# A new order for the attention's steps, and one norm's gain product cut between POOL and VectorE

## The chip, the cores and the metric

The kernel runs on one core of a Trainium2 chip. The metric is the device time of one execution in microseconds (us); lower is better. Engines are written as in the profile: PE is TensorE's matmul, PEld its weight load, DVE is VectorE, ACT is ScalarE, POOL is GpSimd, SP is SyncE, which issues the DMAs.

## The reference, cut to what matters

Input and output are 256 rows of 1024 float32. Two layers run in turn; each has a half SwiGLU block (an FFN of width 2816), a mixer, and another half SwiGLU block, each with a norm in front and a norm behind:

```
for i in range(2):
    f = swiglu(rms_norm(x, g[0]), ...);            x = x + 0.5 * rms_norm(f, g[1])
    h = rms_norm(x, g[2])
    m = pool_mixer(h, ...) if i == 0 else nsa_mixer(h, ...)
    x = x + rms_norm(m, g[3])
    f = swiglu(rms_norm(x, g[4]), ...);            x = x + 0.5 * rms_norm(f, g[5])
```

`rms_norm(x, g)` is `x * rsqrt(mean(x*x) + eps) * g`. The mixer of layer 0 is linear in h up to a bias (causal means over 2, 4, 8 and 16 rows, then a product with a 256 x 256 matrix for each of four groups of columns), so that the row factor of its norm may be multiplied in later. The mixer of layer 1 is an attention with 16 heads in 4 groups: one projection of h gives queries, three pairs of keys and values, and gates; one pair is compressed (blocks of 32 rows through a small two-layer network), and each query attends to the compressed keys, to selected blocks and to a window. At 256 rows all blocks are selected, so the second and the third branch are plain causal softmaxes. The three outputs are weighted by the gates and projected.

## The kernel before, in words

The 256 rows are two tiles of 128 rows, t = 0 and 1. Weights come from HBM as float32 pieces (`raw`, four buffers of 128 x 1024). Each is split in two float32r parts, `hi` by a copy on ACT (L295) and `lo` by a subtraction on VectorE (L296); a product takes three matmuls, hi by hi, hi by lo and lo by hi (`mm3`, L304 to L307). The weight tiles `whi` and `wlo` have three buffers, so the next piece can be split only when a matmul group has let one go.

The stages follow each other in `_trunk`: `ffn`, `pool_mixer`, `ffn`, `ffn`, `nsa`, `ffn`. In front of each stands an object of the class `Pre` (L369 to L401), which makes the normed and transposed input of the stage for each row tile. `Pre(2, False)` belongs to the pooling mixer: it multiplies x by the gain alone (`scaled`, L355, two halves of 512 columns, both on VectorE, L358), computes the row factor `r` beside it (`rstd`), and transposes on PE (L365); `r` is applied after the group matmuls (L606, L607). The others multiply by gain and row factor in one instruction a half (L394). `post` (L345) is the norm behind a stage; its L351 writes x half by half.

The attention stage, `nsa`, is a list of steps, `NSA_STEPS`, each a kind with two indices, which `step` (L950) carries out by tracing instructions. The kinds that matter here:

- `load c h` brings half h of projection chunk c and splits it; `proj c t` multiplies it by row tile t (24 matmuls). Chunks 3 and 5 are the queries, 4 the values of the two plain branches.
- `q c t` copies eight heads' queries out of PSUM (L783); `nope c t` transposes them (L789); `rope c t` rotates their first 16 columns in place by small VectorE operations (L683 to L688), splits them in hi and lo (L311) and transposes both (L803). The writes of L687 and L688 wait for the transposes of `nope`, which read the same tile.
- `cmp`, `hid`, `kcmp`, `vcmp` compress keys and values. `cmp_mm` is 64 small matmuls in the trace (L745); `cmp_k` ends with two VectorE copies to `kbd` (L766); `cmp_v` starts with two copies to `rep` (L772). `pc c t` is the softmax over compressed keys (L814 on), `pct` its transpose.
- `qk t g` is the plain softmax of group g, in four calls: scores of two heads' two branches and their exponentials, then a scaling, then both again for the other two heads. A score step takes two of the four PSUM banks called `acc`: scores and mask on PE (L855, L857), maximum on VectorE (L859), exponentials on ACT (L861), which set the banks free. The scaling is on POOL (L869, L870).
- `pv t g` transposes the weights (L893) and multiplies them by the values (L880), with a masked copy on POOL (L906).
- `wo i` brings a quarter of the output projection and splits it in four pieces of 512 columns: hi on ACT, lo on POOL (`eng=nc.gpsimd`, L988). `out t h` multiplies by it.

What sets the order: the code is traced once, and a planner (`schedule_with_timeline_sim=True`) lays the instructions out on each engine. It runs through its own estimate of the times; at each point an engine gets, of the instructions whose inputs and buffers its estimate has ready, the one that was traced first. The place in `NSA_STEPS` is thus a priority, not the place on the engine. On the chip each engine works off its queue in the order that the planner left, and waits at an instruction whose inputs are late, with all that stands behind it. Blocks under `urgent` have a raised priority, and `after` adds an order by hand.

Of the kernel before, what the change touches and what calls it, by code (L numbers as in the profile page):

```python
# [13 lines left out]
OP = mybir.AluOpType  # L14
# [22 lines left out]
NSA_STEPS = [  # L37
    ("kpost", 0, 0),
    ("load", 1, 0),
    ("wcmp", 0, 0),  # L40
    ("load", 1, 1),
    ("load", 4, 0),
    ("cpost", 0, 0),
    ("load", 4, 1),
    ("load", 3, 0),
    ("proj", 0, 1),
    ("proj", 1, 0),
    ("proj", 4, 0),
    ("cpost", 0, 1),
    ("load", 3, 1),  # L50
    ("kpost", 0, 1),
    ("proj", 1, 1),
    ("cmp", 0, 0),
    ("proj", 3, 0),
    ("cpost", 1, 0),
    ("cpost", 1, 1),
    ("proj", 4, 1),
    ("gates", 0, 0),
    ("q", 0, 0),
    ("load", 5, 0),  # L60
    ("hid", 0, 0),
    ("nope", 0, 0),
    ("proj", 3, 1),
    ("wcmp", 1, 0),
    ("vpost", 0, 1),
    ("cmp", 1, 0),
    ("kcmp", 0, 0),
    ("pc", 0, 0),
    ("q", 0, 1),
    ("rope", 0, 0),  # L70
    ("load", 5, 1),
    ("proj", 5, 0),
    ("nope", 0, 1),
    ("qk", 0, 0),
    ("hid", 1, 0),
    ("qk", 0, 0),
    ("pc", 0, 1),
    ("q", 1, 0),
    ("pct", 0, 0),
    ("proj", 5, 1),  # L80
    ("qk", 0, 1),
    ("rope", 0, 1),
    ("qk", 0, 1),
    ("vcmp", 0, 0),
    ("qk", 0, 0),
    ("qk", 1, 1),
    ("qk", 0, 0),
    ("q", 1, 1),
    ("qk", 1, 0),
    ("nope", 1, 0),  # L90
    ("pct", 0, 1),
    ("vpost", 0, 0),
    ("pv", 0, 0),
    ("nope", 1, 1),
    ("qk", 1, 0),
    ("pc", 1, 0),
    ("rope", 1, 0),
    ("pv", 0, 0),
    ("pv", 0, 0),
    ("qk", 0, 1),  # L100
    ("pc", 1, 1),
    ("qk", 0, 1),
    ("pv", 0, 1),
    ("pct", 1, 0),
    ("qk", 1, 0),
    ("pv", 0, 1),
    ("qk", 0, 2),
    ("qk", 1, 0),
# [5 lines left out]
    ("rope", 1, 1),
    ("vcmp", 1, 0),
    ("qk", 1, 1),
    ("pv", 1, 0),
    ("qk", 1, 1),
    ("qk", 0, 3),
    ("qk", 1, 1),  # L120
    ("pv", 1, 1),
    ("pv", 1, 0),
    ("pv", 1, 1),
    ("qk", 0, 2),
    ("qk", 0, 3),
    ("wo", 0, 0),
    ("qk", 0, 2),
    ("qk", 1, 2),
    ("qk", 1, 3),
    ("qk", 1, 3),  # L130
    ("pv", 1, 1),
    ("qk", 0, 2),
    ("pv", 1, 1),
    ("qk", 0, 3),
    ("pv", 0, 2),
    ("pct", 1, 1),
    ("out", 0, 0),
    ("pv", 0, 2),
    ("pv", 1, 1),
    ("qk", 1, 2),  # L140
    ("qk", 1, 3),
    ("qk", 1, 2),
    ("pv", 0, 3),
# [3 lines left out]
    ("pv", 0, 2),
    ("qk", 1, 2),
    ("wo", 1, 0),
    ("pv", 0, 3),  # L150
# [3 lines left out]
    ("out", 0, 1),
    ("pv", 1, 2),
    ("wo", 2, 0),
    ("pv", 1, 2),
    ("wo", 3, 0),
    ("pv", 1, 3),
    ("pv", 1, 2),  # L160
# [77 lines left out]
def _trunk(ctx: ExitStack, tc: tile.TileContext, d, out):  # L238
    nc = tc.nc
# [5 lines left out]
    x = [pp.tile([P, DM], F32, name=f"x{t}") for t in range(NT)]  # L245
# [11 lines left out]
    rope = csm[:, 290:322].rearrange("p (t n) -> p t n", t=NT)  # L257
# [11 lines left out]
    H = [slice(h * 512, (h + 1) * 512) for h in range(2)]  # L269
# [61 lines left out]

    def rstd(src, half, t):
        s = pp.tile([P, 2], F32, name=f"ssq{t}", bufs=2)
        k = 4.0 if half else 1.0
        for h in range(2):
            j = pp.tile([P, 512], BF16, name="junk", bufs=1)
            nc.scalar.activation(j, src[h], AF.Square,
                                 scale=(2.0 if half else 1.0) / 32.0, accum_out=s[:, h:h + 1])
        v = pp.tile([P, 1], F32, name=f"ms{t}", bufs=2)
        nc.vector.tensor_scalar(v, s[:, 0:1], s[:, 1:2], EPS * k, op0=OP.add, op1=OP.add)  # L340
        r = pp.tile([P, 1], F32, name=f"rs{t}", bufs=2)
        nc.gpsimd.tensor_tensor(r, v, neghalf, op=OP.pow)  # L342
        return r
# [8 lines left out]
            if last:  # L352
                nc.sync.dma_start(out[t * P:(t + 1) * P, H[h]], x[t][:, H[h]])

    def scaled(t, g):  # L355
        xg = fx[t]
        for h in range(2):
            nc.vector.tensor_mul(xg[:, H[h]], x[t][:, H[h]], g[:, H[h]])  # L358
        return xg

    def transposeT(src, dst):
        for h in range(2):
            pt = psG.tile([P, 4, P], F32, name="g")
            for k in range(4):
                i = nc.tensor.transpose(pt[:, k, :], src[:, (4 * h + k) * P:(4 * h + k + 1) * P], ident)  # L365
            r = split([q[:, 4 * h:4 * h + 4, :] for q in dst], pt)
        return r, i

    class Pre:  # L369
        def __init__(self, n, normed=True):  # L370
            self.n, self.normed, self.g, self.xT, self.xx, self.r, self.h, self.T = n, normed, None, None, None, {}, {}, {}

        def load(self):
# [3 lines left out]
        def emit(self, t):  # L377
            if t in self.r:
                return
            self.load()  # L380
            if self.xT is None:
                self.xx = pp.tile([P, 2, KD, S], F32R, name="xT")
                self.xT = tuple(self.xx[:, i] for i in range(2))
            with urgent(t):
                if self.n == 0:
                    self.r[t] = r = rstd(halves(x[t]), False, t)
                    xg = fx[t]
                    self.s = [nc.vector.scalar_tensor_tensor(xg[:, H[h]], x[t][:, H[h]], r, self.g[h], op0=OP.mult, op1=OP.mult)
                              for h in range(2)]
# [653 lines left out]
```

## Time and profile before

| | |
|---|---|
| median of 3 runs | 943.79 us (943.63 to 943.89) |
| the profiled execution | 944.33 us, of it 942.5 us span |
| busy in the span | PE 922.8, PEld 771.4, DVE 634.5, ACT 466.2, POOL 84.3 us |
| granted TensorE clock | 0.996 of full speed |

The span runs from the first to the last instruction that the profiler recorded. Busy time is the union of the instructions of an engine; what is left of PE's span, 19.7 us, are its waits. The order of the stages in the span, read off the lines in the timeline: the first FFN to about 198 us, the pooling mixer to 213, the next two FFNs to 584, the attention to 750, and the last FFN.

### The profile page before, as it was taken

What the parts mean: (1) busy time and instruction counts of PE and PEld (TensorE: products, weight loads), DVE (VectorE), ACT (ScalarE), POOL (GpSimd) and SP (SyncE); (2) the same over time, 40 slices, a digit from 0 to 9 for tenths busy, and PEclk for the clock granted to TensorE, in tenths of its full rate; (3) what the DMA queues carried; (4) which work ended last, traced back from release to release, by engine and by line L of the source; (5) the groups of instructions that cost most, each with busy time, mean ns of one, the idle gap of its engine ahead of it and who ended that gap; (6) DMA issues with size and microseconds to landing.
All of it is one profiled execution on the core that took longest, in us unless ns stands there. A gap on an engine that the chain in (4) does not pass through costs nothing.

```text
span 942.5 us, 13047 instructions
## 1 busy us (share of the span) xinstructions
PE 922.8 (98%) x4922; PEld 771.4 (82%) x4922; DVE 634.5 (67%) x899; ACT 466.2 (49%) x792; POOL 84.3 (9%) x104
## 2 busy tenths in 40 slices
PE   8999999999999999999999999999899999999997
PEld 5888888877888888878888888877776688888886
DVE  5866776786867667558576666775863668666653
ACT  6643644364744444446454444544874565544421
POOL 0003000110000000000000000002667100000000
PEclk9999999999999999999999999999899999999999
DMA  8865765334866656248665662835200358665511
GB/s 317 287 217 165 261 225 183 110 131 157 269 244 192 206 175 224 97 133 277 217 223 180 195 207 63 307 140 179 90 1 27 107 190 296 204 211 185 188 45 45
DMA packets 48021, 168.96 MB, mean 179 GB/s; under 512 B 5587, under 2 KB 6099, under 8 KB 47958
## 3 DMA queue, kind: packets, MB, share of 16 engines
q1 hardware_dynamic: 47958, 168.12, 53.4%
q8 instruction: 39, 0.64, 0.3%
q14 instruction: 24, 0.20, 0.1%
HBM read 167.05 MB, written 1.05 MB: 178 GB/s over the span
## 4 chain that ended last, share of the span: by engine, by line
PE 94%; DVE 3%; ACT 2%; issue 1%; DMA 0%; POOL 0%; DVEq 0%; POOLq 0%; SPq 0%; ACTq 0%
PE g L504 28%; PE g L505 15%; PE acc L305 9%; PE acc L307 9%; PE acc L306 9%; PE g L305 5%; PE g L306 5%; PE g L307 5%; PE g L472 2%; PE g L365 1%; PE g L880 1%; PE g L893 1%; PE g L745 1%; PE acc L855 1%; ACT big L861 1%
## 5 line engine op out<-in xcount | busy, mean ns | idle before, releaser
L504 PE MATMUL g<-xT,whi 128*128 128x512 f32 x1152 | 406.1, 394 | 0.0
L505 PE MATMUL g<-xT,wlo 128*128 128x256 f32 x1152 | 325.1, 282 | 0.0
L295 ACT ACTIVATE whi<-raw 128x1024 fp32r<-128x1024 f32 (+2 forms) x252 | 204.8, 862 | 159.1 <-issue 43.3
L296 DVE TENSOR_TENSOR wlo<-raw,whi 128x1024 fp32r<-128x1024 f32 (+2 forms) x236 | 230.8, 1020 | 47.5 <-ACT whi L295 47.1
L504 PEld LDWEIGHTS g<-xT,whi 128*128 128x128 f32 x1152 | 216.3, 188 | 49.6
L505 PEld LDWEIGHTS g<-xT,wlo 128*128 128x128 f32 x1152 | 216.5, 188 | 1.4
L296 DVE TENSOR_TENSOR dlo<-raw,dhi 128x1024 fp32r<-128x1024 f32 (+1 forms) x128 | 119.4, 954 | 95.3 <-ACT dhi L295 95.2
L295 ACT ACTIVATE dhi<-raw 128x1024 fp32r<-128x1024 f32 (+1 forms) x128 | 103.9, 841 | 146.2 <-DMA raw<-in_wd 140.9
L441 DVE TENSOR_REDUCE sg<-g 128x256 f32<-128x512 f32 x144 | 98.1, 686 | 59.7 <-PE g L505 59.5
L305 PE MATMUL acc<-dhi,hTh 128*128 128x512 f32 x288 | 112.3, 390 | 0.0
L306 PE MATMUL acc<-dlo,hTh 128*128 128x512 f32 x288 | 112.1, 389 | 0.0
L307 PE MATMUL acc<-dhi,hTl 128*128 128x512 f32 x288 | 111.5, 389 | 0.0
L342 POOL TENSOR_TENSOR rs<-ms,neghalf 128x1 f32<-128x1 f32 x24 | 13.2, 549 | 618.5 <-DVE ms L340 618.5
L305 PE MATMUL g<-whi,xT 128*128 128x512 f32 (+2 forms) x168 | 65.1, 388 | 0.8 <-ACT xT L310 0.8
L306 PE MATMUL g<-wlo,xT 128*128 128x512 f32 (+2 forms) x168 | 64.2, 382 | 0.0
L307 PE MATMUL g<-whi,xT 128*128 128x512 f32 (+2 forms) x168 | 63.5, 380 | 0.0
L307 PEld LDWEIGHTS acc<-dhi,hTl 128*128 128x128 f32 x288 | 54.1, 188 | 11.2
L305 PEld LDWEIGHTS acc<-dhi,hTh 128*128 128x128 f32 x288 | 54.0, 188 | 11.3
L306 PEld LDWEIGHTS acc<-dlo,hTh 128*128 128x128 f32 x288 | 54.0, 188 | 10.0
L310 ACT ACTIVATE hTh<-sg 128x512 fp32r<-128x512 f32 x36 | 22.3, 619 | 34.1 <-DVE sg L444 34.1
L305 PEld LDWEIGHTS g<-whi,xT 128*128 128x128 f32 x168 | 32.2, 192 | 7.8 <-ACT xT L310 1.9
L306 PEld LDWEIGHTS g<-wlo,xT 128*128 128x128 f32 x168 | 32.1, 191 | 6.6 <-DVE wlo L296 0.7
(173 smaller groups left out, 980.0 us busy)
## 6 DMA issues: line engine op xcount, KB each, us to landing
raw<-in_wu SPq DMA_DIRECT2D x88, 512.0 KB, 4.6
raw<-in_wd SPq DMA_DIRECT2D x88, 512.0 KB, 4.6
raw<-in_wg SPq DMA_DIRECT2D x86, 512.0 KB, 3.8
raw<-in_win SPq DMA_DIRECT2D x18, 512.0 KB, 4.2
gain<-in_gains SPq DMA_DIRECT2D x11, 512.0 KB, 4.5
raw<-in_wo SPq DMA_DIRECT2D x8, 512.0 KB, 4.1
big<-in_wk SPq DMA_DIRECT2D x4, 512.0 KB, 6.8
big<-in_wv SPq DMA_DIRECT2D x4, 512.0 KB, 5.0
```

The source lines that it names most:

```text
L295: nc.scalar.activation(hi[:, n + a:n + b], r[:, a:b], AF.Copy)
L296: (eng or nc.vector).tensor_tensor(lo[:, n + a:n + b], r[:, a:b], hi[:, n + a:n + b].bitcast(F32), op=OP.subtract)
L305: nc.tensor.matmul(o, A[0], B[0], start=start, stop=False)
L306: nc.tensor.matmul(o, A[0], B[1], start=False, stop=False)
L307: return nc.tensor.matmul(o, A[1], B[0], start=False, stop=stop)
L310: return (nc.scalar.activation(dst[0], src, AF.Copy), nc.vector.tensor_tensor(dst[1], src, dst[0].bitcast(F32), op=OP.subtract))
L342: nc.gpsimd.tensor_tensor(r, v, neghalf, op=OP.pow)
L365: i = nc.tensor.transpose(pt[:, k, :], src[:, (4 * h + k) * P:(4 * h + k + 1) * P], ident)
L441: nc.vector.tensor_reduce(dst, o.rearrange("p a b -> p b a"), axis=AX.X, op=OP.add)
L472: nc.tensor.matmul(o, A(t, k)[i], B[k][j], start=n == 0, stop=n == len(its) - 1)
L504: nc.tensor.matmul(o, hi, pre.xx[:, :, k, :], start=k == 0, stop=False)
L505: nc.tensor.matmul(o[:, 1, :], lo, xT[0][:, k, :], start=False, stop=k == KD - 1)
```

## The change

Two edits. The first puts the same 128 entries of `NSA_STEPS` in another order. Entries written kind and indices, as `qk01` for `("qk", 0, 1)`; before:

```
kpost00 load10 wcmp00 load11 load40 cpost00 load41 load30 proj01 proj10 proj40 cpost01 load31 kpost01 proj11 cmp00
proj30 cpost10 cpost11 proj41 gates00 q00 load50 hid00 nope00 proj31 wcmp10 vpost01 cmp10 kcmp00 pc00 q01
rope00 load51 proj50 nope01 qk00 hid10 qk00 pc01 q10 pct00 proj51 qk01 rope01 qk01 vcmp00 qk00
qk11 qk00 q11 qk10 nope10 pct01 vpost00 pv00 nope11 qk10 pc10 rope10 pv00 pv00 qk01 pc11
qk01 pv01 pct10 qk10 pv01 qk02 qk10 pv10 pv10 pv01 pv10 qk03 rope11 vcmp10 qk11 pv10
qk11 qk03 qk11 pv11 pv10 pv11 qk02 qk03 wo00 qk02 qk12 qk13 qk13 pv11 qk02 pv11
qk03 pv02 pct11 out00 pv02 pv11 qk12 qk13 qk12 pv03 pv03 qk13 out10 pv02 qk12 wo10
pv03 pv12 pv12 pv13 out01 pv12 wo20 pv12 wo30 pv13 pv12 out02 pv13 out03 pv13 pv13
```

and after:

```
kpost00 load10 cpost00 wcmp00 load40 load11 load41 proj11 proj10 load30 proj01 cpost01 proj40 kpost01 cmp00 load31
proj30 proj41 cpost11 proj31 hid00 cpost10 kcmp00 q00 load50 gates00 nope00 wcmp10 cmp10 pc00 load51 rope00
qk00 qk01 hid10 qk01 vpost00 q01 proj50 q10 nope01 pct00 pc01 nope10 proj51 vcmp00 pct01 rope01
rope10 qk00 qk01 qk11 qk00 qk10 qk02 qk00 vpost01 qk10 q11 qk01 nope11 vcmp10 pc10 qk10
wo00 pv00 qk10 qk11 rope11 pv01 pv00 qk11 pv00 pv10 qk12 pc11 pv01 pv01 pv10 qk12
qk02 pct10 pv10 qk03 pv10 pv10 qk03 qk11 qk13 qk03 qk02 pv11 wo10 qk02 qk13 qk03
pv02 pv11 pv11 wo20 pct11 pv03 pv03 pv02 pv02 out00 qk12 pv11 qk12 pv12 qk13 pv03
qk13 pv13 pv12 out10 pv13 pv11 pv12 wo30 pv12 pv12 out01 pv13 out02 pv13 out03 pv13
```

The second edit gives `Pre` a flag `split`, set for the pooling mixer's norm alone. With it, the product of x and gain has its first half on POOL and its second on VectorE, for both row tiles. The further branch, in which a split norm multiplies by `r` in an instruction of its own, is not entered: the flag's only user has `normed` false.

```diff
-    def scaled(t, g):
+    def scaled(t, g, both):
         xg = fx[t]
         for h in range(2):
-            nc.vector.tensor_mul(xg[:, H[h]], x[t][:, H[h]], g[:, H[h]])
+            eng = nc.gpsimd if both and h == 0 else nc.vector
+            eng.tensor_tensor(xg[:, H[h]], x[t][:, H[h]], g[:, H[h]], op=OP.mult)
         return xg
...
-                elif self.normed:
+                elif self.normed and not self.split:
...
-                    xg = scaled(t, self.g)
+                    xg = scaled(t, self.g, self.split)
                     self.r[t] = r = rstd(halves(x[t]), False, t)
+                    if self.normed:
+                        for h in range(2):
+                            nc.vector.tensor_scalar(xg[:, H[h]], xg[:, H[h]], r, None, op0=OP.mult)
...
-    pre = [Pre(0), Pre(2, False), Pre(4), Pre(6), Pre(8), Pre(10)]
+    pre = [Pre(0), Pre(2, False, True), Pre(4), Pre(6), Pre(8), Pre(10)]
```

## Rows read from the trace of the kernel before

**Rows 1.** The page's granted clock in 40 slices, and its chain that ended last.

```profile
PEclk9999999999999999999999999999899999999999
...
PE 94%; DVE 3%; ACT 2%; issue 1%; DMA 0%; POOL 0%; DVEq 0%; POOLq 0%; SPq 0%; ACTq 0%
```

**Rows 2.** PE's waits, whole span: total us, times, longest us.

```profile
PE acc L855 <- ACT big L861: 3.6, 1, 3.6
...
PE g L365 <- DVE fx L394: 1.5, 1, 1.5
...
PE g L789 <- ACT y L783: 0.7, 1, 0.7
```

**Rows 3.** Windows: length, busy PE, PEld, DVE, ACT, POOL, PEclk, DMA share, GB/s.

```profile
650.00:700.00 50.00, 43.90 (x274) 36.34 (x276) 35.20 (x91) 34.00 (x129) 33.54 (x41) 0.93 0.21 65
...
675.00:680.00 5.00, 2.47 (x14) 2.18 (x14) 5.00 (x10) 3.60 (x15) 3.13 (x4) 0.85 0.67 210
680.00:685.00 5.00, 4.55 (x18) 4.16 (x19) 3.08 (x9) 4.47 (x19) 1.40 (x2) 0.50 0.00 2
```

**Rows 4.** PE's timeline in the attention: start us, duration us, line, tiles, count, wait.

```profile
645.69 3.71 PE L745 MATMUL g<-big 128*64 128x128 f32 x64
...
651.38 1.05 PE L814 MATMUL g<-kbd,y 128*128 128x32 f32 x8 [1.39 <-DVE kbd L766]
...
667.25 0.28 PE L855 MATMUL acc<-kTh,q 128*128 128x256 f32 x1
...
667.97 1.03 PE L803 MATMUL g<-csm,q 128*128 128x128 f32 x8
668.84 0.56 PE L774 MATMUL g<-wv,rep 128*128 128x64 f32 x4
669.24 0.61 PE L789 MATMUL g<-csm,y 128*128 128x128 f32 x4
670.05 0.50 PE L855 MATMUL acc<-kTh,q 128*128 128x512 f32 x1 [0.21 <-DVE q L808]
...
671.42 0.50 PE L855 MATMUL acc<-kTh,q 128*128 128x512 f32 x1
...
677.48 0.39 PE L855 MATMUL acc<-kTh,q 128*128 128x256 f32 x1 [3.64 <-ACT big L861]
```

**Rows 5.** VectorE's timeline, same columns, 662 and 670 to 677 us.

```profile
662.12 0.21 DVE L688 TENSOR_TENSOR y<-rB,rA 128x64 f32<-128x64 f32 x1
...
670.05 1.53 DVE L772 COPY rep<-hidT 128x128 f32<-128x128 f32 x2
...
671.86 1.33 DVE L688 TENSOR_TENSOR y<-rB,rA 128x64 f32<-128x64 f32 x1
673.22 1.27 DVE L685 TENSOR_TENSOR rA<-rV,csm 128x128 f32<-128x128 f32 x1
...
675.69 1.27 DVE L859 TENSOR_REDUCE ast<-acc 128x2 f32<-128x512 f32 x2
```

**Rows 6.** POOL's timeline, 672 to 677 us.

```profile
671.81 5.08 POOL L296 TENSOR_TENSOR wlo<-raw,whi 128x512 fp32r<-128x512 f32 x4
```

**Rows 7.** ACT by line and form, 655 to 735 us: count, busy us, mean ns, idle before.

```profile
L861 ACT ACTIVATE big<-acc,ast 128x256 f32<-128x256 f32 x32 | 14.8, 481 | 11.0 <-DVE ast L859 11.0
...
L861 ACT ACTIVATE big<-acc,ast 128x128 f32<-128x128 f32 x32 | 11.5, 388 | 0.8 <-DVE ast L859 0.7
```

**Rows 8.** Timelines of VectorE and PE in front of the pooling mixer, t = 0.

```profile
192.11 1.42 DVE L351 SCALAR_TENSOR_TENSOR x<-fx,rs,x 128x512 f32<-128x512 f32 x2
193.44 1.29 DVE L358 TENSOR_TENSOR fx<-x,gain 128x512 f32<-128x512 f32 x2
...
194.27 1.23 PE L365 MATMUL g<-csm,fx 128*128 128x128 f32 x8 [0.40 <-DVE fx L358]
```

**Rows 9.** Timelines of POOL and VectorE at 740 us.

```profile
740.05 1.05 POOL L906 TENSOR_TENSOR PT<-Pc,csm 128x512 f32<-128x512 f32 x1
...
740.12 1.53 DVE L351 SCALAR_TENSOR_TENSOR x<-fx,rs,x 128x512 f32<-128x512 f32 x1
```

More of the change, by code (lines that the diff above doesn't have):

```diff
@@ L39 @@
     ("load", 1, 0),
+    ("cpost", 0, 0),
     ("wcmp", 0, 0),
+    ("load", 4, 0),
     ("load", 1, 1),
-    ("load", 4, 0),
-    ("cpost", 0, 0),
     ("load", 4, 1),
+    ("proj", 1, 1),
+    ("proj", 1, 0),
     ("load", 3, 0),
     ("proj", 0, 1),
-    ("proj", 1, 0),
+    ("cpost", 0, 1),
     ("proj", 4, 0),
-    ("cpost", 0, 1),
+    ("kpost", 0, 1),
+    ("cmp", 0, 0),
     ("load", 3, 1),
-    ("kpost", 0, 1),
-    ("proj", 1, 1),
-    ("cmp", 0, 0),
     ("proj", 3, 0),
+    ("proj", 4, 1),
@@ L55 @@
+    ("cpost", 1, 1),
+    ("proj", 3, 1),
+    ("hid", 0, 0),
     ("cpost", 1, 0),
-    ("cpost", 1, 1),
-    ("proj", 4, 1),
-    ("gates", 0, 0),
+    ("kcmp", 0, 0),
     ("q", 0, 0),
     ("load", 5, 0),
-    ("hid", 0, 0),
+    ("gates", 0, 0),
     ("nope", 0, 0),
-    ("proj", 3, 1),
     ("wcmp", 1, 0),
-    ("vpost", 0, 1),
     ("cmp", 1, 0),
-    ("kcmp", 0, 0),
     ("pc", 0, 0),
+    ("load", 5, 1),
+    ("rope", 0, 0),
+    ("qk", 0, 0),
+    ("qk", 0, 1),
+    ("hid", 1, 0),
+    ("qk", 0, 1),
@@ L69 @@
+    ("vpost", 0, 0),
     ("q", 0, 1),
-    ("rope", 0, 0),
-    ("load", 5, 1),
     ("proj", 5, 0),
+    ("q", 1, 0),
     ("nope", 0, 1),
-    ("qk", 0, 0),
[L75 to L80, printed above, removed]
+    ("pct", 0, 0),
+    ("pc", 0, 1),
+    ("nope", 1, 0),
+    ("proj", 5, 1),
+    ("vcmp", 0, 0),
+    ("pct", 0, 1),
+    ("rope", 0, 1),
+    ("rope", 1, 0),
+    ("qk", 0, 0),
     ("qk", 0, 1),
-    ("rope", 0, 1),
@@ L83 @@
-    ("qk", 0, 1),
-    ("vcmp", 0, 0),
-    ("qk", 0, 0),
     ("qk", 1, 1),
     ("qk", 0, 0),
+    ("qk", 1, 0),
+    ("qk", 0, 2),
+    ("qk", 0, 0),
+    ("vpost", 0, 1),
+    ("qk", 1, 0),
     ("q", 1, 1),
+    ("qk", 0, 1),
+    ("nope", 1, 1),
+    ("vcmp", 1, 0),
+    ("pc", 1, 0),
     ("qk", 1, 0),
-    ("nope", 1, 0),
-    ("pct", 0, 1),
-    ("vpost", 0, 0),
+    ("wo", 0, 0),
     ("pv", 0, 0),
-    ("nope", 1, 1),
     ("qk", 1, 0),
-    ("pc", 1, 0),
-    ("rope", 1, 0),
+    ("qk", 1, 1),
@@ L98 @@
+    ("rope", 1, 1),
+    ("pv", 0, 1),
     ("pv", 0, 0),
+    ("qk", 1, 1),
     ("pv", 0, 0),
-    ("qk", 0, 1),
+    ("pv", 1, 0),
+    ("qk", 1, 2),
     ("pc", 1, 1),
-    ("qk", 0, 1),
     ("pv", 0, 1),
+    ("pv", 0, 1),
+    ("pv", 1, 0),
+    ("qk", 1, 2),
+    ("qk", 0, 2),
     ("pct", 1, 0),
[L105 to L108, printed above, removed]
+    ("pv", 1, 0),
+    ("qk", 0, 3),
     ("pv", 1, 0),
     ("pv", 1, 0),
-    ("pv", 0, 1),
-    ("pv", 1, 0),
-    ("qk", 0, 3),
@@ L114 @@
[L114 to L118, printed above, removed]
     ("qk", 0, 3),
     ("qk", 1, 1),
[L121 to L124, printed above, removed]
+    ("qk", 1, 3),
     ("qk", 0, 3),
[L126 to L131, printed above, removed]
     ("qk", 0, 2),
     ("pv", 1, 1),
+    ("wo", 1, 0),
+    ("qk", 0, 2),
+    ("qk", 1, 3),
     ("qk", 0, 3),
     ("pv", 0, 2),
+    ("pv", 1, 1),
@@ L136 @@
+    ("pv", 1, 1),
+    ("wo", 2, 0),
     ("pct", 1, 1),
+    ("pv", 0, 3),
+    ("pv", 0, 3),
+    ("pv", 0, 2),
+    ("pv", 0, 2),
     ("out", 0, 0),
-    ("pv", 0, 2),
+    ("qk", 1, 2),
     ("pv", 1, 1),
     ("qk", 1, 2),
+    ("pv", 1, 2),
     ("qk", 1, 3),
-    ("qk", 1, 2),
-    ("pv", 0, 3),
     ("pv", 0, 3),
     ("qk", 1, 3),
+    ("pv", 1, 3),
+    ("pv", 1, 2),
     ("out", 1, 0),
[L147 to L150, printed above, removed]
+    ("pv", 1, 3),
+    ("pv", 1, 1),
@@ L151 @@
+    ("pv", 1, 2),
+    ("wo", 3, 0),
     ("pv", 1, 2),
     ("pv", 1, 2),
+    ("out", 0, 1),
     ("pv", 1, 3),
[L154 to L160, printed above, removed]
     ("out", 0, 2),
@@ L163 @@
     ("out", 0, 3),
-    ("pv", 1, 3),
     ("pv", 1, 3),
@@ L369, in _trunk, with __init__ @@
     class Pre:
-        def __init__(self, n, normed=True):
+        def __init__(self, n, normed=True, split=False):
+            self.split = split
             self.n, self.normed, self.g, self.xT, self.xx, self.r, self.h, self.T = n, normed, None, None, None, {}, {}, {}
```

## The prediction

> **What bounds the kernel now.** I read the page's chain first, then PE's list of waits, then windows over the stage that the list points to, and last the timelines of the engines inside that stage. The chain says what to ask: 94% of the span is PE's own work [rows 1], so only what PE waits, and the clock at which it runs, can move the time; the number of matmuls stays the same in this change. The list of waits [rows 2] shows two in the attention: 3.6 us in front of a score matmul (L855) for exponentials, and 0.7 us in front of `nope` for the copy of the first queries; the timeline adds 1.39 us in front of `pc` for `kbd` [rows 4]. A further one, 1.5 us for L394, is the end of the pooling mixer, which the second edit precedes. The windows [rows 3] show a second loss that no list of waits holds: of 50 us from 650 to 700 PE is busy 43.9, at a mean granted clock of 0.93, and the clock is at 0.50, the lower level (1.2 GHz), from 680 to 685, just behind the long wait. Taking 1 minus the granted clock times 5 us, the two windows lose 0.75 and 2.5 us: 3.25 us. PE had stood still for 3.64 us before the clock fell; the waits of 1.39 and 1.5 us lie in slices whose digit is 9 [rows 1].
>
> The timelines tell where the 3.64 us come from. PE issued the scores that it had until the four `acc` banks were full, the last at about 673, and then stood until 677.48 for an exponential [rows 4]. The exponential stood behind a maximum (L859), and that one was not late by itself: VectorE worked off small operations first [rows 5]. L688, 0.21 us when it is alone, took 1.33; L685, an operation of much the same size, 1.27; the two copies to `rep` 1.53. All the while POOL split the `wo` pieces, 1.27 us each (5.08 for four) [rows 6]. So a small VectorE operation lasts about as long as one POOL subtraction beside it; the maxima, which read PSUM, do not (1.27 us for two, 0.64 each).
>
> **The change, part by part.** The sum is made against the profiled execution, 944.33 us, 942.5 of it span; what lies around the span, 1.83 us, I leave alone. The median of the runs is 943.79, 0.54 lower, and I take that off at the end.
>
> *The wait at `nope00`, 0.7 us* [rows 2]. Before, `q00` and `nope00` stand ahead of `proj31`, so PE comes to the transposes straight behind the projection whose result ACT still has to copy. After, `proj31` stands ahead of both: 24 matmuls cover the copy. If the planner keeps them apart, minus 0.7; if not, nothing. I take minus 0.7.
>
> *The wait at `pc00`, 1.39 us* [rows 4]. Before, the list has `cmp10 kcmp00 pc00`, and PE does the three back to back, so the copies to `kbd` lie bare. After it has `kcmp00 q00 load50 gates00 nope00 wcmp10 cmp10 pc00`: the 3.71 us of L745 [rows 4] stand between. Minus 1.39; if `cmp10` still comes first, nothing.
>
> *The wait at the scores, 3.64 us.* `nope10` moves ahead of `proj51`, so the in-place writes of `rope10` (L687, L688) can run while PE still does that projection, before the `wo` splits begin: L688's excess of 1.33 - 0.21 = 1.12 us goes from in front of the maximum [rows 5]. What stays: the copies to `rep` need `vcmp00`'s matmul, which still follows `proj51`, and L685, with L686 behind it, is that of `rope11`, as late as before. The POOL work stays too: the splits of `wo` start when `proj51` lets weight buffers go, and it does so in both lists. Bounds: 0 and the whole 3.64; I take minus 1.12, the one operation whose place the list clearly moves.
>
> *The clock, 3.25 us* [rows 3]. With 1.12 us less the wait would be 2.5 us. It lies between one that cost no clock (1.5) and one that did (3.64); the new list also mixes the steps around it anew, so that it is unlikely to stay in one piece. Bounds 0 and minus 3.25; I take minus 3.25, and the chance below says how sure.
>
> *Five score steps in a row.* Behind `rope10` the list now has `qk01 qk11 qk00 qk10 qk02`, three of t = 0 and two of t = 1, all of which issue scores. PE takes 0.72 us for one of t = 0 (667.25 to 667.97) and 1.37 for one of t = 1 (670.05 to 671.42) [rows 4]: 4.9 us. ACT takes four exponentials each, 0.388 or 0.481 us [rows 7]: 3 x 1.55 + 2 x 1.92 = 8.5 us. With two steps' banks in all, PE waits for the difference, 3.6 us, less what else it can do: `vcmp10`, `nope11` and `pc10` stand right behind, 0.56 + 0.61 + 1.05 = 2.2 us by their rows (L774, L789, L814) [rows 4]. Bounds 0 and 3.6; I take plus 1.4, in several short waits.
>
> *The gain product on POOL, t = 0.* VectorE's first half ends now at 193.44 + 0.64 = 194.08, and PE has waited 0.40 us for it [rows 8]: nothing covers a delay. POOL can start once the first half of x is written, at 192.11 + 0.71 = 192.82. Its price has no row of the same form; a product of 128 x 512 with a broadcast operand took 1.05 [rows 9], a subtraction of two full tensors 1.27 [rows 6]. If it ran beside VectorE it would end at 193.87 to 194.09, a gain of at most 0.2. But VectorE's L351 took 1.53 beside a POOL product at 740 [rows 9] and 0.71 without one [rows 8], so the two don't run side by side. Then POOL follows the second L351, which ends at 193.53: 194.80, plus 0.7; and VectorE's own half follows POOL, 195.45, 0.7 later than now too. If VectorE takes both its instructions first, POOL ends at 195.45, plus 1.4. Bounds minus 0.2 and plus 1.4; I take plus 0.7.
>
> On this the Trainium skill ("SBUF — State Buffer", section "Who interferes with whom") says that a VectorE instruction with two SBUF inputs and a GpSimd instruction that reads SBUF exclude each other, that the one that starts first holds the port for its whole length, and that the other is blocked fully. The row at 740 nearly shows it: the VectorE instruction lost 0.82 us of the 0.98 that POOL's had left [rows 9]. By the full block the sum below stands; by the row VectorE's half would end 0.16 us earlier, and the sum would be 939.3.
>
> *The same, t = 1.* PE has other work there, and the first wait behind it is the 1.5 us for L394 [rows 2]. VectorE is freed of 0.64 us, half of L358's two [rows 8], and may be blocked by up to 1.3. Bounds minus 0.6 and plus 1.3; I take 0.
>
> *The rest.* The loads come in another order (`load40` before `load11`), but the same pieces through the same weight buffers, and SP's queue carries the same DMAs; `wo10` and `wo20` move ahead of some `pv` and `out` steps, but before they were split long ahead of their place already, as soon as buffers were free [rows 6]. At the end one `pv13` less stands between `out03` and the last norm; three `out` steps of t = 1 stay behind it as cover. I take 0, and price what speaks against it as a rival.
>
> Sum: -0.7 - 1.39 - 1.12 - 3.25 + 1.4 + 0.7 = -4.36. 944.33 - 4.36 = 939.97, and less 0.54: **939.4 us**.
>
> **The rivals.**
> *A. The stall stays where it is.* The list gives priorities only, and the planner fills by readiness: all of `wo` stands far down in the old list, and a quarter of it was still split at 672 [rows 6]. The VectorE queue may again have `rope` and `rep` in front of the maxima. For it: `rep` and L685 keep their place by the list. Against it: `rope11` is lower in the list than three more score calls. Then the 1.12 and the 3.25 are not won: -0.7 - 1.39 + 1.4 + 0.7 = 0.0, 944.3, by the median 943.8. That is no change.
> *B. POOL gets in the way, slower.* `wo00` now stands ahead of the first `pv`, `wo10` and `wo20` ahead of the last ones. If the planner puts four splits, 5.08 us in a row [rows 6], in front of a scaling (L870) or a masked copy (L906) that the next `pv` on PE needs, PE stands for them on top of A: 944.33 + 0.0 + 5.08 - 0.54 = 948.9 if nothing covers it. It decides where PE has less than 5.08 us of other work queued ahead of that `pv`; the 2.2 us of small steps above are the likeliest cover, which gives 946.7. For it: from 650 to 700 POOL is busy for 33.5 of 50 us [rows 3]. Against it: the splits are ready no earlier than before.
>
> **How the numbers follow.** I call a change of under 0.2%, 1.9 us, none: a measurement of this kernel can't tell less. My forecast has 0.52, A 0.22, B 0.26. The forecast's own range is 935.5 (the whole 3.64 won, the new short waits covered for the most part) to 942.0 (four fifths of the clock lost again). Faster: 0.49 of the forecast's 0.52 and a quarter of A's, 0.54. Slower: most of B, 0.25. The rest, 0.21, is no change. The range reaches from 935.0, where nearly all waits of the stage are gone, to 947.5, past B with its cover.
>
> **What would show it.** Right: no window between 650 and 700 with a granted clock under 0.9; the wait of L814 for `kbd` and that of L789 for the copy gone; the longest wait of L855 under 2 us; L688 at 0.2 us in front of the scores; PE's wait for the transposes at 194 us at about 1.1 us. Wrong: a wait of over 3 us of PE anywhere in the attention with the lower clock behind it, or a row of four L296 on POOL with PE waiting for what follows it.

## The result, and the profile after

The kernel with the change takes 939.04 us (938.70 to 939.71, median of 4 runs), the kernel before beside it 943.77 (943.63 to 943.89): a ratio of 0.9945 [0.9932, 0.9957], 4.7 us or 0.5% faster. The forecast was 939.4. The time is right, the way to it is not: of the sum's terms two came as forecast and one near it, four did not, and one that the sum doesn't hold makes up for them. Runs of one kernel lie at two levels near 2 us apart (before at 943.0 to 944.4 and 945.1 to 946.4 us, the split alone, below, at 942.0 to 943.2 and 944.1 to 945.0, about 1.0 us lower at either), which the batches of runs mix differently, so that the ratios below are each against a mixture of its own.

The profiled execution took 939.71 us, 937.9 of it span (line numbers above 400 are 5 higher than before: L855 is now L860, L861 is L866, L808 is L813). The page's busy line, its granted clock in 40 slices and its chain, which answer to [rows 1]:

```profile
PE 918.1 (98%) x4922; PEld 771.3 (82%) x4922; DVE 635.1 (68%) x897; ACT 466.7 (50%) x792; POOL 87.3 (9%) x106
...
PEclk9999999999999999999999999999899999999999
...
PE 94%; DVE 2%; ACT 2%; DMA 1%; issue 1%; POOL 0%; SPq 0%; DVEq 0%; POOLq 0%; ACTq 0%
```

PE's busy time fell from 922.8 to 918.1, though it does the same matmuls. Of the span's 4.6 us PE thus gave back 4.7 by working less, and its waits are what they were (19.7 and 19.8 us). The slice with an 8 in the clock is still there. (The attention's waits grew and the pooling mixer's shrank; the table below parts them.) PE's waits, whole span, against [rows 2] (total us, times, longest us):

```profile
PE acc L860 <- DVE q L813: 5.2, 1, 5.2
...
PE g L706 <- ACT fx L702: 1.4, 1, 1.4
...
PE g L750 <- issue: 1.1, 1, 1.1
PE g L366 <- POOL fx L359: 0.8, 1, 0.8
```

The waits for `kbd` (1.39) and at `nope` (0.7) are gone, and so is the 1.5 at the end of the pooling mixer; but the stall in front of the scores grew from 3.6 to 5.2 us, now for a VectorE copy of rotated queries. The windows around it, as in [rows 3] (length, busy PE, PEld, DVE, ACT, POOL, PEclk, DMA share, GB/s):

```profile
650.00:700.00 50.00, 44.15 (x275) 36.91 (x273) 34.90 (x91) 35.43 (x135) 30.31 (x38) 0.93 0.16 50
...
670.00:675.00 5.00, 1.65 (x4) 1.36 (x5) 3.27 (x4) 0.66 (x2) 5.00 (x5) 0.65 0.72 220
675.00:680.00 5.00, 4.66 (x27) 4.13 (x26) 3.63 (x7) 3.59 (x17) 0.09 (x1) 0.67 0.38 127
```

The lower level of the clock (0.5 of full speed, 1.2 GHz) is there as before, with a mean of 0.93 over the 50 us. It lasts 6.83 us in both kernels, but now begins at 671.5, while PE is still waiting, so that PE works 4.62 us at the lower level instead of 6.32. The timelines of PE, VectorE and POOL say why PE waits; they answer to [rows 4 to 6] (start us, duration us, line, tiles, count, wait):

```profile
667.07 1.06 PE L808 MATMUL g<-csm,q 128*128 128x128 f32 x8
673.36 0.80 PE L860 MATMUL acc<-kTh,q 128*128 128x512 f32 x1 [5.23 <-DVE q L813]
```

```profile
662.60 0.21 DVE L693 TENSOR_TENSOR y<-rB,rA 128x64 f32<-128x64 f32 x1
...
667.29 1.61 DVE L777 COPY rep<-hidT 128x128 f32<-128x128 f32 x2
668.83 1.30 DVE L688 COPY rV<-y 128x128 f32<-128x128 f32 x1
670.16 1.27 DVE L690 TENSOR_TENSOR rA<-rV,csm 128x128 f32<-128x128 f32 x1
671.36 1.34 DVE L691 TENSOR_TENSOR rB<-rV,csm 128x128 f32<-128x128 f32 x1
672.62 0.68 DVE L813 CAST q<-g 128x512 fp32r<-128x512 f32 x1
```

```profile
665.02 10.06 POOL L296 TENSOR_TENSOR wlo<-raw,whi 128x512 fp32r<-128x512 f32 x8
```

POOL now splits eight pieces of `wo` in a row, two quarters of it, in front of the scores. Beside them the operations of L688, L690 and L691 take 1.27 to 1.34 us each on VectorE, about one POOL subtraction (10.06 / 8 = 1.26 us). The operation that the forecast moved is at 662.60, 0.21 us long (L693, once L688); but four others now stand in its place, and PE stands behind the copy that follows them.

To see where PE worked less, cut the span at matmuls. Mixer: from the last L505 of the first FFN (182.71 us before) to the first product of the next FFN, so that it takes in the end of the first FFN. Attention: from PE's first transpose of its input to the first product of the FFN behind it. "Waits" is the sum of PE's waits over 0.04 us in it, "low" PE's busy time at the lower clock; "own" is the stage less the waits and less half of "low". At half the clock a matmul takes at most twice as long, so half is an upper bound for what the clock costs, and own times are compared only between kernels that have a low stretch, or between those that have none. "Changes" counts how often PE goes between matmuls of 128 x 128 and of 128 x 64 (in the trace 128\*64: the compression, L750, and the weights times values, L885).

| kernel | median us | ratio to before, 95% | mixer | attention | waits | low | own | changes |
|---|---|---|---|---|---|---|---|---|
| before | 943.77 | | 32.01 | 166.72 | 7.56 | 6.32 | 156.00 | 54 |
| after | 939.04 | 0.9945 [0.9932, 0.9957] | 30.84 | 163.57 | 8.37 | 4.62 | 152.89 | 36 |
| new list alone | 939.69 | 0.9951 [0.9939, 0.9963] | 32.07 | 162.48 | 7.91 | 3.28 | 152.93 | 36 |
| split alone | 944.12 | 0.9995 [0.9987, 1.0004] | 30.84 | 166.62 | 7.33 | 6.50 | 156.04 | 54 |
| before, `cmp` in one run | 941.99 | 0.9974 [0.9965, 0.9983] | 32.01 | 164.46 | 6.62 | 5.71 | 154.98 | 48 |
| before, wo 1, 2 on VectorE | 940.99 | 0.9959 [0.9947, 0.9972] | 31.98 | 163.48 | 6.02 | 0 | 157.46 | 56 |
| list, wo 1, 2 on VectorE | 935.59 | 0.9902 [0.9888, 0.9915] | 32.01 | 159.05 | 5.04 | 0 | 154.00 | 38 |
| after, wo 1, 2 on VectorE | 934.85 | 0.9897 [0.9883, 0.9912] | 30.84 | 159.47 | 5.39 | 0 | 154.07 | 38 |
| the same, split for t = 1 only | 934.74 | 0.9895 [0.9880, 0.9910] | 30.37 | 158.29 | 4.28 | 0 | 154.01 | 38 |
| the same, `pv` grouped | 935.11 | 0.9901 [0.9886, 0.9916] | 30.34 | 158.51 | 5.47 | 0 | 153.05 | 28 |
| after, wo 1, 2 later | 938.67 | 0.9945 [0.9933, 0.9957] | 30.84 | 159.88 | 7.47 | 0 | 152.40 | 34 |

The FFNs agree within 0.2 us, the head (up to the mixer's cut) within 1.0, but for the last FFN of the last two rows. Of the 4.6 us, 1.17 are the mixer's, 3.15 the attention's, 0.3 the head's. In the attention the waits grew by 0.8, the low clock costs at most 0.85 less, and PE's own time fell by 3.1. That is the term which the forecast lacks. (The two kernels' low stretches differ; with the same two lists and no low stretch, further down, own time falls by 3.46.)

### The profile page after: what moved, and what is told of

Read it like the earlier page. It is cut to its first block, busy times and chain, and to the rows that moved or that the text cites. A ratio compares the mean times of both kernels' runs of the same rounds, so it can differ in the third digit from the quotient of the medians.

```text
span 937.9 us, 13055 instructions
## 1 busy us (share of the span) xinstructions
PE 918.1 (98%) x4922; PEld 771.3 (82%) x4922; DVE 635.1 (68%) x897; ACT 466.7 (50%) x792; POOL 87.3 (9%) x106
## 3 DMA queue, kind: packets, MB, share of 16 engines
HBM read 167.05 MB, written 1.05 MB: 179 GB/s over the span
## 4 chain that ended last, share of the span: by engine, by line
PE 94%; DVE 2%; ACT 2%; DMA 1%; issue 1%; POOL 0%; SPq 0%; DVEq 0%; POOLq 0%; ACTq 0%
PE g L509 28%; PE g L510 15%; PE acc L305 9%; PE acc L307 9%; PE acc L306 9%; PE g L305 4%; PE g L306 4%; PE g L307 4%; PE g L477 2%; PE g L885 2%; PE acc L860 1%; PE g L898 1%; PE g L366 1%; PE g L750 1%; ACT whi L295 1%
## 5 line engine op out<-in xcount | busy, mean ns | idle before, releaser
L296 DVE TENSOR_TENSOR wlo<-raw,whi 128x1024 fp32r<-128x1024 f32 (+2 forms) x236 | 230.8, 1020 | 51.1 <-ACT whi L295 50.2
L296 DVE TENSOR_TENSOR dlo<-raw,dhi 128x1024 fp32r<-128x1024 f32 (+1 forms) x128 | 119.4, 955 | 93.4 <-ACT dhi L295 92.8
L307 PE MATMUL acc<-dhi,hTl 128*128 128x512 f32 x288 | 111.5, 389 | 0.0
L307 PE MATMUL g<-whi,xT 128*128 128x512 f32 (+2 forms) x168 | 63.4, 379 | 0.0
L307 PEld LDWEIGHTS acc<-dhi,hTl 128*128 128x128 f32 x288 | 54.0, 188 | 11.3
L305 PEld LDWEIGHTS g<-whi,xT 128*128 128x128 f32 x168 | 31.9, 190 | 7.6 <-ACT xT L310 1.9
L307 PEld LDWEIGHTS g<-whi,xT 128*128 128x128 f32 x168 | 32.0, 191 | 6.6 <-DVE xT L311 0.7
```

The source lines that it names most:

```text
L296: (eng or nc.vector).tensor_tensor(lo[:, n + a:n + b], r[:, a:b], hi[:, n + a:n + b].bitcast(F32), op=OP.subtract)
L305: nc.tensor.matmul(o, A[0], B[0], start=start, stop=False)
L307: return nc.tensor.matmul(o, A[1], B[0], start=False, stop=stop)
```

## The experiments

**Which edit does it.** Two kernels, each with one of the two edits: the list `NSA_STEPS` alone, or the flag `split` alone.

```diff
-    pre = [Pre(0), Pre(2, False), Pre(4), Pre(6), Pre(8), Pre(10)]
+    pre = [Pre(0), Pre(2, False, True), Pre(4), Pre(6), Pre(8), Pre(10)]
```

> The new list of steps alone, the gain product left on VectorE. Theory: the two edits lie in stages that don't touch, so this gives what the attention gained between the two traces (584.17 to 750.89 us before, 582.70 to 746.27 after: 166.72 to 163.57, 3.15 us) and nothing of the pooling mixer: 940.6 us, ratio 0.9967; PE still waits some 5.2 us for the copy at L808 of the old numbering, with the lower clock behind it. Rival: the list won what I forecast, 5 us, and the split lost some: 938.7. A second rival: the planner lays the attention out otherwise when what comes before it is shifted by a microsecond, and the 3.15 us are luck of that shift: 943 to 944.

> The split gain product alone, with the old list. Theory: the transposes of t = 0 start 0.45 us later as in the trace of the changed kernel (they wait 0.84 instead of 0.40 us for the product), and the wait of 1.5 us for L394 at the end of the mixer goes, since the planner puts the squares of ACT in another order; together 1.2 us faster, 942.6, ratio 0.9988. Rival, from my forecast: only the delay is real, 0.4 to 0.7 us slower, 944.3.

The list alone took 939.69 us, 0.9 less than expected: its attention is 162.48 us long and not 163.57. The split alone took 944.12, no change by the time, and its median alone would fit the rival; but its mixer, 30.84 against 32.01, shows the 1.17 us. So the attention's gain is the list's, the mixer's is the split's, and neither needs the other. Together the attention keeps 1.1 us less than the list alone gives; of this 0.46 are waits, and PE works 4.62 us at the lower clock instead of 3.28.

**What makes the stall.** In the first kernel the `lo` parts of the second and third quarter of `wo` are made on VectorE, so that POOL has nothing beside the rotation; in the second POOL keeps them, ordered behind two scalings of the softmax.

```diff
-  wo.append(ksplit(piece(d["wo"][:, i * 2048:(i + 1) * 2048], step=512, eng=nc.gpsimd), 2))
+  wo.append(ksplit(piece(d["wo"][:, i * 2048:(i + 1) * 2048], step=512, eng=nc.vector if i in (1, 2) else nc.gpsimd), 2))
```

```diff
-  nc.gpsimd.tensor_tensor(pe[:, :, :nk], pe[:, :, :nk], r[:, :, None].to_broadcast([P, 4, nk]), op=OP.mult)
+  scaled_at[t, g, pr] = nc.gpsimd.tensor_tensor(pe[:, :, :nk], pe[:, :, :nk], r[:, :, None].to_broadcast([P, 4, nk]), op=OP.mult)
...
-  wo.append(ksplit(piece(d["wo"][:, i * 2048:(i + 1) * 2048], step=512, eng=nc.gpsimd), 2))
+  with after([scaled_at[k] for k in {1: [(1, 1, 1)], 2: [(0, 3, 1)]}.get(i, [])]):
+      wo.append(ksplit(piece(d["wo"][:, i * 2048:(i + 1) * 2048], step=512, eng=nc.gpsimd), 2))
```

> The changed kernel, but the lo parts of the second and third quarter of wo are subtracted on VectorE instead of POOL. Theory (POOL's subtractions block the small VectorE operations): the copies to rep and the rope operations fall back to 0.2 to 0.35 us each, 4.2 us earlier, and the wait of 5.2 us of PE for the second copy of the rotated queries shrinks to about 1 us; VectorE has 8 x 0.65 = 5.2 us of subtractions more, which stand in front of maxima, so that a part comes back as a wait for exponentials: 935 to 938. Rival (VectorE has simply too many operations there, POOL has no part in it): the small operations keep their 1.3 us, and 5.2 us more of work make the wait longer: 944 or more.

> The changed kernel, with the second and third quarter of wo ordered on POOL behind later scalings of the softmax (the one of t = 1, group 1, second pair, and that of t = 0, group 3, second pair), so that POOL is free of them while rope and the first scores run. Theory (POOL's subtractions block the small VectorE operations): the wait of 5.2 us for the copy of the rotated queries shrinks to 1 us or less, the clock stays at its upper level, and 4.2 + 2.5 us are won: 932 to 934. It fails where out steps then wait for wo. Rival (the four banks and ACT bound the stretch): the same microseconds come back a few steps later as waits of the scores for exponentials: 938 to 940.

With VectorE doing the two quarters the time is 934.85 us, a little under the 935 to 938 expected. VectorE's timeline of this kernel in front of the same copy, and PE's behind it:

```profile
664.40 2.71 DVE L296 TENSOR_TENSOR wlo<-raw,whi 128x512 fp32r<-128x512 f32 x4 [0.33 <-ACT whi L295]
...
667.16 0.35 DVE L777 COPY rep<-hidT 128x128 f32<-128x128 f32 x2
667.43 0.21 DVE L688 COPY rV<-y 128x128 f32<-128x128 f32 x1
...
668.34 0.28 DVE L690 TENSOR_TENSOR rA<-rV,csm 128x128 f32<-128x128 f32 x1
668.54 0.29 DVE L691 TENSOR_TENSOR rB<-rV,csm 128x128 f32<-128x128 f32 x1
668.74 0.68 DVE L813 CAST q<-g 128x512 fp32r<-128x512 f32 x1
```

```profile
669.48 0.50 PE L860 MATMUL acc<-kTh,q 128*128 128x512 f32 x1 [1.59 <-DVE q L813]
```

The same four lines take 0.35 + 0.21 + 0.28 + 0.29 = 1.13 us instead of 1.61 + 1.30 + 1.27 + 1.34 = 5.52, though VectorE now does the splits as well, at 0.68 us each where POOL takes 1.26. The wait falls to 1.59, and the clock stays up, as the window shows:

```profile
650.00:700.00 50.00, 47.00 (x297) 38.68 (x295) 37.58 (x102) 37.09 (x144) 23.20 (x33) 1.00 0.15 49
```

So 3.6 of the stall's 5.2 us are POOL's subtractions beside VectorE's small operations, and the low clock comes with the stall: it fell in all five kernels whose longest wait of the attention is 3.6 us or more, and in none of the six where it is 1.6 or less. What lies between no run here shows.

The later splits keep the clock up too, with a wait of 0.8 us at L860. But the time is 938.67, where 932 to 934 was expected; it lies in the rival's 938 to 940. The attention has new waits of 0.6 to 1.1 us (at L898, L885, L307, and L860 for exponentials), and the last FFN's matmuls take 188.30 us instead of 185.58, about 1.9 of it by eight matmuls (0.23 each) that the count shows missing from the attention, 990 for 998 (with them its own time is about 154.3, no less than with VectorE, though its part of the attention has four changes fewer). Attention and last FFN together are 348.2 us, against 345.05 with VectorE and 349.15 with the change as it was: most of the gain was turned into other waits.

**Is the list's gain the stall's shape, or PE's own time?** Old and new list, both with `wo` 1 and 2 on VectorE (the edit above) and both without the split.

> The kernel before with the lo parts of wo 1 and 2 on VectorE; old order, no split. Theory (the port, and changes of the PE array): the 3.64 us stall and the low clock behind it go, 3.64 + half of 6.32 = 6.8 us, so the attention falls from 166.7 to about 160 and the time from 943.8 to about 937. PE's own time in the attention (without waits over 40 ns and without low clock) stays at about 156.0, with some 54 changes between matmuls of 128 and of 64 columns. Rival (the new order won its 3 us through the shape of the stall alone): without a stall the old order is as good as the new, own time 153 to 154 as in the run with the new order, attention 157 to 158, time about 934.5. If the stall stays, the port is not its cause under the old order: about 943.8.

> The new order with wo 1 and 2 on VectorE, no split at all. Theory: the split is worth its 1.2 us in the mixer and up to 0.3 in front of it whatever the attention does: mixer 32.0, time 936.0 to 936.4 against 934.85 with the split. The attention keeps 36 to 38 changes of the array and an own time of PE of 153 to 154, against about 156.0 in the kernel with the old order and the same wo. Rival: the split's worth is an accident of the stage's clock, and the two kernels agree within 0.4 us.

The stall and the low clock are gone from both; the attention takes 163.48 us with the old list and 159.05 with the new one. The list is worth 4.43 us without a stall, 4.24 with it (166.72 to 162.48). Own time falls by 3.46, waits by 0.98. The old list came out 3 to 4 us slower than expected: its own time is 157.46 and not 156.0, it keeps the waits for `kbd` and at `nope`, and new waits stand in the stall's place (7.56 us of waits became 6.02, though 3.64 went). What is left of the gain for the low clock is 3.24 - 1.54 = 1.7 us, about half of the bound of 3.16. The rival is out: the new order's gain is not a better-placed stall. The split is worth 0.7 us here by the medians (935.59 to 934.85, the intervals overlap), between the 1.2 and the at most 0.4 of the two expectations, and 1.17 by the mixer.

**Which half of the split.** The kernel at 934.85 with POOL's half for row tile 1 alone.

```diff
-            eng = nc.gpsimd if both and h == 0 else nc.vector
+            eng = nc.gpsimd if both and h == 0 and t == 1 else nc.vector
```

> The new order, wo 1 and 2 on VectorE as in the run at 934.85, and the product of x and gain on POOL only for row tile 1 (for row tile 0 both halves on VectorE). Theory: for row tile 0 the POOL half only costs, PE's wait for the transposes at 194 us falls from 0.84 back to 0.40; the 1.5 us gained at the end of the mixer comes from row tile 1: mixer 30.4, time 934.4. Rival: the planner's order at the end of the mixer comes with row tile 0's half (ACT's squares are laid out otherwise); then the 1.5 us wait for the normed halves comes back: mixer 32.0, time 936.

> The same kernel as the run with the split for row tile 1 alone, to compare on one chip with the one that groups pv: 934.7, attention 158.3, mixer 30.4, 38 changes of the array.

934.74 and, in a second set of runs, 934.42 us; the mixer is 30.37 and 30.38, the wait for the transposes at 194 us back at 0.4, and there is no wait at the end of the mixer. So the half for row tile 1 brings the gain, 1.64 us of the mixer with the wait of 1.5 in it, and the half for row tile 0 costs 0.47 of it. By the time alone the kernels with one and with both halves can't be told apart. This is the fastest version here: 0.9893 [0.9880, 0.9907] of before.

**What a change of the width costs, by itself.** This kernel leaves the model out and runs matmuls alone, all in float32, with all operands ready and the clock at full speed; `half` is a matmul with weights of 128 x 64 (one half of the array's columns, the two halves by turns), `whole` one with 128 x 128, `T` a transpose. The whole is done three times:

```
for f in (half, whole):
    for k in (4, 24):
        for _ in range(24 // k):
            T(k)
            f(k)
        warm(4)
```

> None of the model is computed. After 160 matmuls of 128x512 that bring the clock up, PE does 24 transposes (128x128 f32) and 24 matmuls of 256 f32 columns, in fours by turns or in one run of 24 each, once with weights of 128x64 (half of the array) and once with weights of 128x128. All operands are ready. Theory (a change between half and whole array costs 0.10 to 0.17 us beyond what a change of operation costs): in fours with 128x64 there are 12 changes in place of 2, so 1.0 to 1.7 us more than in runs of 24; with 128x128 the two layouts differ by less than 0.3 us. Rival (only the change between transpose and matmul costs, or nothing does): both widths show the same difference.

PE's timeline: the last of six rounds in fours with 64 columns, the same work as two runs of 24, and the rounds in fours with 128 columns (each f32 matmul of `half` and `whole` has two records):

```profile
94.34 0.66 PE L267 MATMUL pt<-csm 128*128 128x128 f32 x4
94.92 1.08 PE L272 MATMUL o<-PT,V 128*64 128x256 f32 x8
95.94 1.20 PE L263 MATMUL acc<-m,w 128*128 128x512 f32 x4
96.97 2.78 PE L267 MATMUL pt<-csm 128*128 128x128 f32 x24
99.69 5.40 PE L272 MATMUL o<-PT,V 128*64 128x256 f32 x48
105.02 1.19 PE L263 MATMUL acc<-m,w 128*128 128x512 f32 x4
106.05 0.60 PE L267 MATMUL pt<-csm 128*128 128x128 f32 x4
106.48 1.89 PE L277 MATMUL o<-PT,F 128*128 128x256 f32 x8
108.21 0.60 PE L267 MATMUL pt<-csm 128*128 128x128 f32 x4
```

A round in fours with 64 columns takes 95.94 - 94.34 = 1.60 us; the same work in one run takes (105.02 - 96.97) / 6 = 1.34. From first transpose to the next L263 the six rounds take 9.546 us and the two runs 8.042, in the second and the third of three repetitions within 0.004 (in the first the planner cut the rounds up): 1.504 us for ten changes more, 0.150 each. With 128 columns it is 12.806 and 12.794. So it isn't the change from transpose to product, nor the alternation, but the change of the array's width.

**The same inside the kernel.** One kernel makes `pv` transpose all four blocks of row tile 1 before it multiplies (on top of the fastest version); another, on the kernel before, puts the `cmp` matmuls in one run.

```diff
+                qs_ = []
                 for n in range(0, len(blocks), 2):
-                    qs_ = []
...
                     yield
-                    for i, (br, kt) in enumerate(blocks[n:n + 2]):
-                        mm(V[:, kt, br, g], qs_[i], n == i == 0, False)
-                    yield
+                for n, (br, kt) in enumerate(blocks):
+                    mm(V[:, kt, br, g], qs_[n], n == 0, False)
+                    if n % 2:
+                        yield
```

```diff
-                    hm[i] = cmp_mm(i, wc[i])
+                    with urgent(0):
+                        hm[i] = cmp_mm(i, wc[i])
```

> The kernel with the new order, wo 1 and 2 on VectorE and the split for row tile 1 alone, with one more edit: for row tile 1 pv transposes all four blocks first and multiplies by the values behind that. By the planned order PE then has 14 runs of 64-column matmuls instead of 19, that is 28 changes of the array instead of 38 in the attention. Theory (0.150 us a change, as alone): PE's own time in the attention 154.0 - 1.5 = 152.5; if the waits stay at 4.3, attention 156.8 and time 933.2 against 934.7. Rival (the correlation with the changes comes from something else in the order): own time stays at 154.0 within 0.3. The edit may cost waits, as the weights' copies come later together; that shows in the waits, not in the own time.

> The kernel before, with the 64 matmuls of the first cmp step under a raised priority, so that they lie in one run and not in four. By the planned order 24 runs of 64-column matmuls instead of 27, so 6 changes of the array less. Theory: PE's own time in the attention 156.0 - 0.9 = 155.1, the rest of the stage as before, time 942.9 against 943.8. Rival: own time stays at 156.0 within 0.2, time 943.8.

With `cmp` in one run: six changes less and 1.02 us less of own time, 0.17 each; the waits fell by 0.9 as well, and the time is 941.99 where 942.9 was expected (the expectation left the waits as they were). With `pv` grouped: ten changes less and 1.03 us, 0.10 each, less than the 1.5 expected; and nothing is won, since the waits grew by 1.1, most of it one new wait of PE for the masked copy, which now stands bare:

```profile
PE g L885 <- POOL PT L912: 0.8, 1, 0.8
```

## Why the prediction was right, and where it was wrong

The total came out by luck. Both signs that the prediction gave for being wrong are there: a wait of over 3 us in the attention with the lower clock at its end, and a row of L296 on POOL with PE waiting for what follows it.

*`nope` and `pc`, -0.7 and -1.39: right.* Both waits are gone, by the covers named: `proj31` behind ACT's copy, and the compression's matmuls behind `kbd`.

*The scores, -1.12, and the clock, -3.25: wrong, and with them two points of "what would show it".* The one operation did move, but the term took for the cause of the stall what was only its place. The cause stood in the same paragraphs, [rows 6] beside [rows 5]: a VectorE operation lasts as long as the POOL subtraction beside it. With the new list the planner laid all eight subtractions of `wo10` and `wo20` in front of the scores, where four had stood. The operations that stood behind the moved one take its place: the wait is 5.23 us, +1.6 instead of -1.12, and the clock gave back at most 0.85. Rival A had VectorE's queue, rival B the row of splits; neither price has the own time of PE. The prices were too high as well: with stall and low clock both gone from the old order, the attention gained 3.24 us and not 3.64 + 3.25.

*Five score steps, +1.4: wrong.* At the scores there is 0.3 us for an exponential. The attention's waits rose by 0.81; -0.7, -1.39 and +1.6 make -0.49, so other new waits are worth +1.3: 1.1 more at L706, 1.1 at L750, less small ones. These stand at the start of the attention, in front of the keys' transposes and of the first compression, and have nothing to do with the five steps; that their sum is near 1.4 is luck.

*The gain product on POOL, +0.7 for t = 0: right in kind, 0.44 in size.* VectorE, POOL and PE there, against [rows 8]:

```profile
193.29 1.65 DVE L359 TENSOR_TENSOR fx<-x,gain 128x512 f32<-128x512 f32 x1
...
192.74 1.65 POOL L359 TENSOR_TENSOR fx<-x,gain 128x512 f32<-128x512 f32 x1 [0.93 <-DVE x L351]
...
194.45 1.27 PE L366 MATMUL g<-csm,fx 128*128 128x128 f32 x8 [0.84 <-POOL fx L359]
```

Once VectorE's second L351 ends (191.84 + 1.42 = 193.26), POOL takes 1.13 us to its end at 194.39, where the forecast had put 1.27; VectorE's own half, 0.64 us alone, takes 1.65 and ends 0.55 behind POOL. They take turns, as the forecast had it; the forecast's sign was a wait of about 1.1 us, and it is 0.84.

*The same for t = 1, 0: wrong, -1.5.* The bounds, -0.6 to +1.3, were drawn from VectorE's and POOL's durations; what moved was ACT's order. After, and before:

```profile
208.22 0.63 ACT L337 ACTIVATE junk<-x 128x512 bf16<-128x512 f32 x1 [0.64 <-DVE x L351]
...
208.97 0.63 ACT L337 ACTIVATE junk<-x 128x512 bf16<-128x512 f32 x1
...
209.60 0.67 ACT L611 ACTIVATE pyh<-acc,rs 128x512 fp32r<-128x512 f32 x1
```

```profile
208.27 0.69 ACT L606 ACTIVATE pyh<-acc,rs 128x512 fp32r<-128x512 f32 x1 [2.32 <-PE acc L307]
208.86 0.62 ACT L337 ACTIVATE junk<-x 128x512 bf16<-128x512 f32 x1
...
209.47 0.68 ACT L606 ACTIVATE pyh<-acc,rs 128x512 fp32r<-128x512 f32 x1
210.04 0.62 ACT L337 ACTIVATE junk<-x 128x512 bf16<-128x512 f32 x1
```

Both squares of the next stage's input now stand ahead of the second L611; the row factor is ready sooner, VectorE's L396 starts at 210.97 instead of 212.58, and PE's wait of 1.51 us is gone. The run with the split for t = 1 alone shows that this half brings it. That it works through ACT's order is read off the traces; no run changed that order alone.

*The term that was left out, -3.1.* The sum treated PE's own time as fixed, since the matmuls are the same. It depends on their neighbours. Before, the first compression lies in four pieces between products, after in one:

```profile
618.76 1.52 PE L745 MATMUL g<-big 128*64 128x128 f32 x22
...
620.64 1.09 PE L745 MATMUL g<-big 128*64 128x128 f32 x16
...
622.93 0.40 PE L305 MATMUL g<-whi,xT 128*128 128x512 f32 x1
623.27 0.66 PE L745 MATMUL g<-big 128*64 128x128 f32 x8
623.85 0.50 PE L306 MATMUL g<-wlo,xT 128*128 128x512 f32 x1
624.19 0.39 PE L307 MATMUL g<-whi,xT 128*128 128x512 f32 x1
...
625.20 1.31 PE L745 MATMUL g<-big 128*64 128x128 f32 x18
```

```profile
621.20 3.71 PE L750 MATMUL g<-big 128*64 128x128 f32 x64
```

The other twelve changes less are in `pv`. 18 times the 0.150 us measured alone is 2.7 of the 3.1; with the 0.10 to 0.17 of the two kernels it is 1.8 to 3.1. Without a low stretch the same 18 changes went with 3.46 us.

The run alone is float32 throughout, but half of the changes (27 of 54 before, 19 of 36 after) lie next to products in float32r, where the operands' format changes with the width. The traces part the two. Take a run between two such products, from the start of the last product in front to the start of the second product behind, less the steady time of the matmuls in it (0.23 us for a product of 512 columns, 0.109 for a transpose, 0.054 for a record of L745, 0.108 for one of the weights times values). Above, L745 x8 has 624.19 - 622.93 - 2 x 0.23 - 8 x 0.054 = 0.37 us over. Eight float32 transposes of the full width have next to nothing over, 585.28 - 583.94 - 2 x 0.23 - 8 x 0.109 = 0.01:

```profile
583.94 0.39 PE L307 MATMUL acc<-dhi,hTl 128*128 128x512 f32 x1
584.17 1.03 PE L365 MATMUL g<-csm,fx 128*128 128x128 f32 x8
584.96 0.48 PE L305 MATMUL acc<-dhi,hTh 128*128 128x512 f32 x1
585.28 0.39 PE L306 MATMUL acc<-dlo,hTh 128*128 128x512 f32 x1
```

Over the attentions of the eleven kernels of the table, where no wait and no low clock is near, 31 runs of 64-column matmuls have 0.35 to 0.47 us over, median 0.36, 0.18 a change; 118 runs of transposes have a median of 0.01. So it is the width and not the format, and next to products a change costs 0.18. With 0.18 for these and 0.150 for the others the 18 changes come to 2.9 us, measured 3.1, and without a low stretch to 3.0, measured 3.46; the six of `cmp` come to 1.05, measured 1.02. The ten of `pv` come to 1.7, measured 1.03; why is open, as is the rest of the 3.46. The trace of before held this: its 54 changes could have been counted, and the 0.37 read off it.

So the total came out because errors of opposite sign cancelled: 1.12 + 1.6 and 2.4 too good at the stall, against 3.1 of own time and 1.5 of row tile 1 that were not in the sum.

## What to carry to other kernels

Where an engine is busy all the time, its busy time is still not a constant: count in the timeline what depends on the order, above all changes between matmuls of different width, and price one by putting the two orders side by side. When a queue of small operations is late because each of them is slow, ask what stretches them and not which one to move; here, when one was moved away, the next took its place. And work that is "off the path" on another engine is cheap only as long as it does not stand beside operations that it holds up.

## What was not expected of the hardware

- Going between transposes of 128 and matmuls of 64 columns cost PE 0.150 us a change, with all operands ready and at a full clock; next to float32r products, in the attention, it was 0.18. The Trainium skill ("TensorEngine Tiling (Array Packing)", section "Key Properties") says that changing the tiling mode drains TensorE. The run alone fits this, with 9.546 us for twelve changes against 8.042 for two; it shows the time, not the drain.
- Beside a row of POOL subtractions, three of VectorE's operations from SBUF (L688, L690, L691) took about one subtraction each, 1.27 to 1.34 us, whether copy or product, against 0.21 to 0.29 without; the cast out of PSUM (L813) took 0.68 with and without. The Trainium skill ("SBUF — State Buffer", section "Who interferes with whom") names copies and two-input operations as those that can contend with GpSimd, and an operation with at most one SBUF input otherwise as free of it; both rows agree.
